# 162 row pairs of the MLP up projections by seven products in place of 120, at other places, in a two-layer decoder trunk

## The chip, the cores and the metric

One core of a Trainium2 chip runs the whole program. The metric is the device time of one execution in microseconds (us). Five engines have queues of their own that run in order: PE (matrix multiply; PEld is its loading of weights), DVE (vector), ACT (scalar), POOL and SP. SP issues almost all DMAs here.

## The reference, cut to what matters

Two layers, 256 tokens, 2048 channels, float32. Each layer is a token mixer (forgetting attention in layer 0, a mixture of dilated windows in layer 1) and an MLP, each behind an RMS norm and added to the residual stream. The change is in the MLPs:

```python
def sq_relu_mlp(h, w_up, w_down):      # h 256 x 2048, w_up 2048 x 8192, w_down 8192 x 2048
    a = jax.nn.relu(h @ w_up)
    return (a * a) @ w_down

h = rms_norm(x, mlp_norm_g[i])
x = x + sq_relu_mlp(h, mlp_w_up[i], mlp_w_down[i])
```

## The kernel before, in words

**Precision.** Each float32 operand is split in two reduced-precision parts, hi and lo (`cut`, L340): ACT casts the weight to hi (L342), DVE subtracts hi from the weight to give lo (L348). A product is three matmuls: hi by hi, hi by lo, lo by hi (L386 to L388).

**Units and blocks.** A `Unit` (L352) is a matrix product of all 256 tokens with 512 columns of a weight; its sums stay in two or four PSUM banks. It runs in eight blocks. A block (L361) is a pair of 128-row chunks of the weight: one 512 KB DMA into a `raw` buffer, a hi and a lo, and PE's work. There are three forms of PE's work:

- `whole` (L376): 12 matmuls of 512 columns.
- `quarters` (L391): the same 12, with the columns in another order, for plain blocks of a unit that also has blocks by seven products.
- `parts` (L410): the 2x2 arrangement (two token halves, two row chunks, two column halves) by seven products in place of eight, 21 matmuls of 256 columns. For this DVE forms sums of weights in a second `raw` buffer (L413, L418, L420), and both the weights (768 columns of them) and the sums (1024 columns) are cut to hi and lo. The sums of tokens (`sigma`, made in `normed` and `sums_of_tokens`) are made once per MLP from each quarter of the normed input.

The table `HALVED` (L42) says for each of the four periods of an MLP and each of the period's four up units which of the eight blocks go by `parts`. Before, it is blocks 0, 2, 4, 5 and 7 in every unit of periods 1 to 3 and none in period 0: 60 pairs per MLP, 120 in all.

**Periods.** In `mlp` (L1016) an MLP is four periods of 2048 of the 8192 inner columns. Period 0 has only four up units. In each later period the four up units alternate with the four down units of the period before, block by block, in an order that a string gives (`UU_D`, L1014: U an up block, D a down block). After the last period come its four down units alone. An up unit ends in `up_end` (L944): ACT moves the banks to a buffer `z` (L968 or L953), DVE adds up the seven products' results there (L973 to L986), ACT applies relu, DVE transposes to `tr` (L994), four DMAs write to DRAM (L448), one reads back into `z` (L453), ACT squares (L1002), and ACT and DVE make hi and lo of the down unit's operand `aT` (L1007, L1009). A down unit ends in an addition to x on DVE (L527).

**Buffers.** They are rings of slots (`Ring`, L62): six `raw`, four `hi`, four `lo`, and in the MLPs more by `MORE` (L41), one of each. `z` has one slot, `tr` four.

**What sets the order.** All steps are recorded with a duration from small formulas (`on_act`, `on_dve`, `moved`, L45 to L54). The planner (`Plan`, L89) plays them through with those durations and hand-over times (`gap`, L137) and emits each engine's instructions in the order that comes out; PE's blocks keep the order in which they were recorded, and steps of attention are set between them. On the chip each engine then runs its own queue in that order.

Of the kernel before, what the change touches and what calls it, by code (L numbers as in the profile page):

```python
# [13 lines left out]
ALU = mybir.AluOpType  # L14
# [3 lines left out]
P = 128  # L18
D = 2048
S = 256  # L20
NT = S // P
NC = 512
# [13 lines left out]
PERIODS = DFF // D  # L36
# [1 line left out]
QUARTER = 0.112  # L38
ADDING = ()
FIVE = (0, 2, 4, 5, 7)  # L40
MORE = (1, 1, 1)  # L41
HALVED = [[(), (), (), ()], [FIVE] * 4, [FIVE] * 4, [FIVE] * 4]  # L42


def on_act(n, accum=False):  # L45
    return 0.24 + 0.00083 * n + (0.19 if accum else 0)


def on_dve(n, inputs=2):
    return 0.17 + (0.00104 if inputs == 2 else 0.00054) * n  # L50


def moved(kb):
    return kb / 380.0  # L54


class Item:
# [31 lines left out]
class Plan:  # L89

    HANDOFF = 0.25
    LANDING = 2.1
    BACKLOG = 2.0
    FIRST = 14.0
# [40 lines left out]
    def gap(self, a, b):  # L137
        if a.eng == "dma":
            return self.LANDING
        if a.eng is None:  # L140
            return 0.0
        if a.eng == b.eng:
            return 0.0 if a.eng == "pe" else 0.06
        return self.HANDOFF

    def order(self, rounds=3):
        for ring in self.rings:
# [81 lines left out]
def trunk(ctx: ExitStack, tc, x, fox_w_in, fox_b_f, fox_q_gain, fox_k_gain, fox_w_out, dil_w_in,  # L229
          dil_q_gain, dil_k_gain, dil_w_out, mix_norm_g, mlp_norm_g, mlp_w_up, mlp_w_down, out):  # L230
    nc = tc.nc
    plan = Plan(["fox", "mlp0", "dil", "mlp1"])
    add = plan.add
    T = {}

    def v(item):
        return T[item.slot if isinstance(item, Item) else item]

    def r(item):
        return v(item).bitcast(F32R)  # L240
# [18 lines left out]
    N_RAW = 6  # L259
    N_HI = 4  # L260
    N_LO = 4
    N_Z = 1
    N_C = 1
    raw_ring = ring("raw", N_RAW, 2 * NC)
# [4 lines left out]
    blocks_ring = Ring(plan, [f"blocks{i}" for i in range(4)])  # L269
    rings = {}  # L270
    for ph in ("mlp0", "mlp1"):
        rings[ph] = dict(sigma=ring("sigma", 4, 2 * 4 * 2 * P, ph), tr=ring("tr", 4, NT * NC, ph),
                         z=ring("z", N_Z, 6 * S, ph), c=ring("c", N_C, NC, ph))
    for ph, n_sets, heads in (("fox", 1, 4), ("dil", 3, 2)):
        rings[ph] = dict(
            s=ring("s", 4, 3 * P, ph), w=ring("w", 4 if ph == "fox" else 3, NT * NC, ph),
# [3 lines left out]
            ph=ring("ph", 2, S, ph), pl=ring("pl", 2, S, ph), pw=ring("pw", 2, P, ph))  # L280
# [194 lines left out]
    def x_keys(n):  # L475
        return [(f"x{n}", t) for t in range(NT)]
# [41 lines left out]
            reads=[room, (sigma, 0)], writes=[(sigma, 1)])  # L518


    def add_to_x(n, then=None):
        def end(banks):
            pair = banks[0].slot[0]

            def go():
# [415 lines left out]
    out_proj(oT, fox_w_out[0], then1)  # L941


    def up_end(l, phase, source, halved):  # L944
        own = rings[phase]

        def end(banks):
            z, turned = own["z"].take(), own["tr"].take()
            by = lambda t: v(f"rstd{l}")[:, t:t + 1]
            if not halved:  # L950
                for t in range(NT):
# [48 lines left out]
            for t in range(NT):  # L1000
# [8 lines left out]
            add("dve", on_dve(2 * NC), lambda: nc.vector.tensor_sub(r(a)[:, 2 * NC:], v(turned), v(a)[:, 0:2 * NC]),  # L1009
                reads=[*((turned, t) for t in range(NT)), *((a, b, 0) for b in range(4))], writes=[(a, b, 1) for b in range(4)])  # L1010
        return end

    AC, BE = ("A0", "A1", "C0", "C1"), ("B0", "B1")
    UU_D = "UUDUDUDUDUDUDUDD"  # L1014

    def mlp(l, layer, phase, source, sigmas, then, last=None):  # L1016
        for weights, name, n in ((raw_ring, "raw", MORE[0]), (hi_ring, "hi", MORE[1]), (lo_ring, "lo", MORE[2])):
            slots = [f"{phase}_{name}{i}" for i in range(n)]
            in_phase[phase].update({s: 2 * NC for s in slots})
            weights.more(slots, phase)  # L1020
        downs = []
        turn = 0
        for b in range(PERIODS):
            a = Source()
            ups = []
            for n in range(4):
                halved = HALVED[b][n]
                banks = AC if halved else ("A0", "A1") if b or n % 2 == 0 else ("B0", "B1")
                ups.append(Unit(source, mlp_w_up[layer], 0, [(b * D + n * NC, NC)], banks,
                                up_end(l, phase, a, halved), halved, sigmas))  # L1030
            if b == 0:
                paired(ups[0], ups[1])
                ups[2].blocks(NP)
                ups[3].blocks(NP)
            else:
                for u, d in zip(ups, downs):
                    for c in UU_D:
                        (u if c == "U" else d).block()
            downs = []
            for n in range(NX):  # L1040
                banks = ("E0", "E1") if turn % 2 == 0 else ("B0", "B1")
                turn += 1
                end = add_to_x(n, then if b == PERIODS - 1 else None)
# [217 lines left out]
```

## Time and profile before

| | |
|---|---|
| median of 3 runs | 2120.92 us (2120.85 to 2121.04) |
| profiled execution | 2121.22 us, of it the span of the program 2119.5 us |
| PE busy | 2109.8 us |
| PEld, DVE, ACT busy | 1888.0, 1669.8, 1266.0 us |
| moved by DMA | 492.93 MB |
| one MLP, periods 0 to 3 | about 381 to 947 us of the span for layer 0 |

The busy time of PE is made of pipelined matmuls whose ends are modelled: a matmul of 512 columns is listed with 379 ns. Its pace is read from the starts in the timeline. In the list of groups, the columns are line, engine, operation, output and inputs, shapes, count, then busy us and mean ns of one, then the engine's idle time before them with what ended it. In a table of windows a cell is busy us and the number of instructions that ran.

### The profile page before, as it was taken

Reading aid. Unit: us, or ns where it says so; the run is one execution under the profiler, and the core shown is the slowest. Engines: PE = TensorE matmul, PEld = TensorE weight load, DVE = VectorE, ACT = ScalarE, POOL = GpSimd, SP = SyncE. Lnnn points to the kernel's source line nnn. Section 1 sums busy time; section 2 is a strip of 40 time slices with the busy share of each in tenths; the row PEclk is TensorE's granted clock in tenths of the full one; section 3 lists DMA queues with packets and bytes.
Section 4 is the critical chain, followed back from the end, with each engine's and each line's share of the span. In section 5 each row is a group of like instructions: output and inputs, shape, how many; then the busy total and the mean of one; then the engine's idle time right before and its main releaser. Section 6 shows DMA issues by size and latency. Waiting matters only on the chain.

```text
span 2119.5 us, 30432 instructions
## 1 busy us (share of the span) xinstructions
PE 2109.8 (100%) x11285; PEld 1888.0 (89%) x11285; DVE 1669.8 (79%) x2092; ACT 1266.0 (60%) x1640; POOL 57.8 (3%) x51
## 2 busy tenths in 40 slices
PE   9999999999999999999999999999999999999999
PEld 7888888889999999998888888888899999999988
DVE  6777777678899899886787777777678898898874
ACT  5555556566666666666555555556666666666652
POOL 1011000000000000000010000000000000000000
PEclk9999999999999999999999999999999999999999
DMA  7777668777767777777786776768767777777773
GB/s 247 233 221 199 212 217 262 240 243 238 228 225 242 241 225 237 245 257 260 227 259 200 235 223 207 249 203 285 237 223 232 249 228 230 248 229 228 248 259 129
DMA packets 336133, 492.93 MB, mean 233 GB/s; under 512 B 21928, under 2 KB 137712, under 8 KB 335984
## 3 DMA queue, kind: packets, MB, share of 16 engines
q1 hardware_dynamic: 335712, 490.86, 72.9%
q8 instruction: 88, 1.44, 0.3%
q14 instruction: 61, 0.50, 0.1%
q10 hardware_dynamic: 272, 0.13, 0.0%
HBM read 455.26 MB, written 35.65 MB: 232 GB/s over the span
## 4 chain that ended last, share of the span: by engine, by line
PE 99%; DMA 0%; SPq 0%; DVE 0%; issue 0%; ACT 0%
PE bank_B L386 11%; PE bank_B L388 11%; PE bank_B L387 11%; PE bank_C L407 9%; PE bank_A L386 7%; PE bank_A L388 7%; PE bank_A L387 7%; PE bank_E L386 7%; PE bank_E L388 7%; PE bank_E L387 7%; PE bank_A L437 3%; PE bank_A L438 3%; PE bank_A L436 3%; PE bank_C L437 2%; PE bank_C L438 2%; PE bank_C L436 2%
## 5 line engine op out<-in xcount | busy, mean ns | idle before, releaser
L342 ACT CAST hi<-raw 128x1024 fp32r<-128x1024 f32 (+1 forms) x720 | 736.0, 1026 | 585.0 <-PE bank_B L388 171.1
L348 DVE TENSOR_TENSOR lo<-raw,hi 128x1024 fp32r<-128x1024 f32 (+1 forms) x720 | 854.7, 1193 | 277.1 <-ACT hi L342 261.7
L386 PE MATMUL bank_A<-hi,hT 128*128 128x512 f32 x552 | 212.0, 384 | 0.0
L388 PE MATMUL bank_A<-hi,hT 128*128 128x512 f32 x552 | 210.3, 381 | 0.0
L387 PE MATMUL bank_A<-lo,hT 128*128 128x512 f32 x552 | 210.2, 381 | 0.0
L386 PE MATMUL bank_B<-hi,aT 128*128 128x512 f32 x520 | 197.5, 380 | 0.5 <-ACT aT L646 0.5
L388 PE MATMUL bank_B<-hi,aT 128*128 128x512 f32 x520 | 197.1, 379 | 0.0
L387 PE MATMUL bank_B<-lo,aT 128*128 128x512 f32 x520 | 197.1, 379 | 0.0
L386 PE MATMUL bank_B<-hi,hT 128*128 128x512 f32 x480 | 183.7, 383 | 0.0
L387 PE MATMUL bank_B<-lo,hT 128*128 128x512 f32 x480 | 181.9, 379 | 0.0
L388 PE MATMUL bank_B<-hi,hT 128*128 128x512 f32 x480 | 181.9, 379 | 0.0
L386 PE MATMUL bank_E<-hi,aT 128*128 128x512 f32 x472 | 179.0, 379 | 0.0
L387 PE MATMUL bank_E<-lo,aT 128*128 128x512 f32 x472 | 178.9, 379 | 0.0
L388 PE MATMUL bank_E<-hi,aT 128*128 128x512 f32 x472 | 178.9, 379 | 0.0
L342 ACT CAST mlp_hi<-raw 128x1024 fp32r<-128x1024 f32 (+1 forms) x108 | 109.7, 1016 | 90.1 <-PE bank_E L388 27.0
L348 DVE TENSOR_TENSOR mlp_lo<-raw,mlp_hi 128x1024 fp32r<-128x1024 f32 (+1 forms) x108 | 127.0, 1176 | 27.7 <-ACT mlp_hi L342 24.1
L407 PE MATMUL bank_C<-hi,hT 128*128 128x512 f32 x430 | 138.5, 379 | 0.0
L388 PEld LDWEIGHTS bank_A<-hi,hT 128*128 128x128 f32 x552 | 104.9, 190 | 15.4 <-DVE hT L711 0.5
L386 PEld LDWEIGHTS bank_A<-hi,hT 128*128 128x128 f32 x552 | 105.1, 190 | 14.0
L387 PEld LDWEIGHTS bank_A<-lo,hT 128*128 128x128 f32 x552 | 105.0, 190 | 14.1
L388 PEld LDWEIGHTS bank_B<-hi,aT 128*128 128x128 f32 x520 | 98.3, 189 | 14.1 <-DVE aT L647 0.2
L386 PEld LDWEIGHTS bank_B<-hi,aT 128*128 128x128 f32 x520 | 98.4, 189 | 13.3 <-ACT aT L646 0.7
(360 smaller groups left out, 4391.7 us busy)
## 6 DMA issues: line engine op xcount, KB each, us to landing
raw<-in_mlp_w_up_dram SPq DMA_DIRECT2D x222, 512.0 KB, 4.5
raw<-in_mlp_w_down_dram SPq DMA_DIRECT2D x222, 512.0 KB, 4.8
raw<-in_fox_w_in_dram SPq DMA_DIRECT2D x96, 512.0 KB, 4.6
raw<-in_dil_w_in_dram SPq DMA_DIRECT2D x192, 256.0 KB, 3.1
blocks<-mlp_tr SPq DMA_DIRECT2D x176, 128.0 KB, 3.6
mlp_z<-blocks SPq DMA_DIRECT2D x44, 512.0 KB, 5.4
mlp_raw<-in_mlp_w_up_dram SPq DMA_DIRECT2D x34, 512.0 KB, 4.5
mlp_raw<-in_mlp_w_down_dram SPq DMA_DIRECT2D x34, 512.0 KB, 4.6
```

The lines of the kernel that those rows point to most:

```text
L342: add("act", on_act(n), lambda: nc.scalar.copy(r(hi)[:, 0:n], v(src)[:, at:at + n]), reads=keys, writes=[hi])
L348: add("dve", on_dve(n), lambda: nc.vector.tensor_sub(r(lo)[:, 0:n], v(src)[:, at:at + n], v(hi)[:, 0:n]), reads=[*keys, hi], writes=[lo])
L386: nc.tensor.matmul(acc, a, h, start=first and i == 0, stop=False)
L387: nc.tensor.matmul(acc, a, l, start=False, stop=False)
L388: nc.tensor.matmul(acc, b, h, start=False, stop=last and i == 1)
L407: nc.tensor.matmul(to, m, w, start=False, stop=False)
L436: nc.tensor.matmul(acc, a(0), w(0, at), start=first and edge & 1 == 1, stop=False)
L437: nc.tensor.matmul(acc, a(0), w(1, at), start=False, stop=False)
L438: nc.tensor.matmul(acc, a(1), w(0, at), start=False, stop=last and edge & 2 == 2)
```

## The change

- `HALVED` is another table. Each MLP now has 81 pairs by seven products, 162 in all: five in the third up unit of period 0, 26 each in periods 1 and 2 (6 or 7 a unit), 24 in period 3 (6 a unit).
- `MORE` goes from (1, 1, 1) to (0, 2, 1): in the MLPs six `raw`, six `hi`, five `lo` slots, where there were seven, five and five.
- `tr` has three slots for four. A new ring `sums` with one slot takes the place of `z` for the up units of period 0 that have no pair by seven products; `z` serves the others.
- `UU_D` is another string: three up blocks stand first, then two down, and three down blocks last.
- The planner's durations are changed (fixed parts of ACT and DVE steps halved, DMAs slower, hand-overs on one engine longer, and 0.2 us or, behind PE, 0.3 us between engines), so the order of all queues is planned anew, in the mixers too.
- Code for additions by DMA is added (`added`, `BY_DMA`, `LOW_BY_DMA`), and switched off.

```diff
-MORE = (1, 1, 1)
-HALVED = [[(), (), (), ()], [FIVE] * 4, [FIVE] * 4, [FIVE] * 4]
+MORE = (0, 2, 1)
+BY_DMA = False
+LOW_BY_DMA = False
+HALVED = [[(), (), (0, 1, 3, 5, 7), ()],
+          [(0, 1, 2, 3, 4, 6, 7), (0, 1, 3, 5, 6, 7), (0, 2, 3, 4, 5, 6, 7), (0, 1, 4, 5, 6, 7)],
...
 def on_act(n, accum=False):
-    return 0.24 + 0.00083 * n + (0.19 if accum else 0)
+    return 0.12 + 0.00083 * n + (0.19 if accum else 0)
...
 def on_dve(n, inputs=2):
-    return 0.17 + (0.00104 if inputs == 2 else 0.00054) * n
+    return 0.085 + (0.00104 if inputs == 2 else 0.00054) * n
...
 def moved(kb):
-    return kb / 380.0
+    return kb / 335.0
...
-    HANDOFF = 0.25
+    HANDOFF = 0.2
...
-            return 0.0 if a.eng == "pe" else 0.06
-        return self.HANDOFF
+            return 0.0 if a.eng == "pe" else 0.12
+        return 0.3 if a.eng == "pe" else self.HANDOFF
...
-        rings[ph] = dict(sigma=ring("sigma", 4, 2 * 4 * 2 * P, ph), tr=ring("tr", 4, NT * NC, ph),
-                         z=ring("z", N_Z, 6 * S, ph), c=ring("c", N_C, NC, ph))
+        rings[ph] = dict(sigma=ring("sigma", 4, 2 * 4 * 2 * P, ph), tr=ring("tr", N_TR, NT * NC, ph),
+                         z=ring("z", N_Z, 6 * S, ph), c=ring("c", N_C, NC, ph), sums=ring("sums", 1, NT * NC, ph))
...
-            add("dma", 0.45, go, reads=[turned], writes=[(blocks, i)])
+            add("dma", 0.5, go, reads=[turned], writes=[(blocks, i)])
...
-            z, turned = own["z"].take(), own["tr"].take()
+            z, turned = own[room].take(), own["tr"].take()
...
-    UU_D = "UUDUDUDUDUDUDUDD"
+    UU_D = "UUUDDUUDUDUDUDDD"
...
-                banks = AC if halved else ("A0", "A1") if b or n % 2 == 0 else ("B0", "B1")
+                banks = (AC if halved else AC[:2]) if b or n % 2 == 0 else BE if halved else BE[:2]
...
-                                up_end(l, phase, a, halved), halved, sigmas))
+                                up_end(l, phase, a, halved, LOW_BY_DMA and n < 3, "z" if b or halved else "sums"), halved, sigmas))
```

Two places of the planned order matter below. The first is on PE, in layer 0's MLP, where the third up unit of period 0 starts (`hT` is the normed input, `mlp_sigma` the sums of tokens). Before:

```order
L388 MATMUL bank_B<-mlp_hi_2630,hT_115 128x512
L386 MATMUL bank_A<-hi_126,hT_112 128x512
L387 MATMUL bank_A<-lo_130,hT_112 128x512
L388 MATMUL bank_A<-hi_126,hT_112 128x512
L386 MATMUL bank_A<-hi_126,hT_112 128x512
```

And with the change:

```order
L394 MATMUL bank_B<-hi_127,hT_115 128x512
L442 MATMUL bank_A<-hi_128,hT_112 128x256
L443 MATMUL bank_A<-lo_130,hT_112 128x256
L444 MATMUL bank_A<-hi_128,hT_112 128x256
L442 MATMUL bank_C<-hi_128,hT_112 128x256
L443 MATMUL bank_C<-lo_130,hT_112 128x256
L444 MATMUL bank_C<-hi_128,hT_112 128x256
L442 MATMUL bank_C<-hi_128,mlp_sigma_2666 128x256
```

The unit's first block is now 21 matmuls of 256 columns and needs the first `sigma` here, two units earlier than before.

The second place is on DVE, in period 1 of the same MLP: from the last reading of a `raw` buffer to the first sum of weights that is read from the buffer's next load. The first row frees the buffer (`raw_122` before), the last reads what was loaded into it meanwhile. Before:

```order
L348 TENSOR_TENSOR lo_132<-raw_122,hi_128 128x1024
L348 TENSOR_TENSOR lo_133<-raw_123,hi_129 128x1024
L418 TENSOR_TENSOR raw_120<-raw_120,raw_125 128x256
L348 TENSOR_TENSOR mlp_lo_2631<-raw_124,mlp_hi_2630 128x1024
L420 TENSOR_TENSOR raw_120<-raw_120,raw_125 128x256
L1009 TENSOR_TENSOR aT_117<-mlp_tr_2624,aT_117 128x1024
L413 TENSOR_TENSOR raw_123<-raw_122 128x512
```

With the change, where the buffer is `raw_121`:

```order
L354 TENSOR_TENSOR mlp_lo_2678<-raw_121,hi_129 128x1024
L419 TENSOR_TENSOR raw_124<-raw_123 128x512
L1004 TENSOR_TENSOR mlp_z_2673<-mlp_z_2673,mlp_c_2674 128x2x256
L1005 TENSOR_TENSOR mlp_z_2673<-mlp_z_2673 128x2x256
L354 TENSOR_TENSOR lo_130<-raw_122,mlp_hi_2676 128x1024
L424 TENSOR_TENSOR raw_124<-raw_124,raw_123 128x256
L419 TENSOR_TENSOR raw_120<-raw_125 128x512
L426 TENSOR_TENSOR raw_124<-raw_124,raw_123 128x256
L354 TENSOR_TENSOR lo_131<-raw_123,mlp_hi_2677 128x768
L424 TENSOR_TENSOR raw_120<-raw_120,raw_125 128x256
L419 TENSOR_TENSOR raw_122<-raw_121 128x512
```

Between the two rows there were five others, three of 1024 columns and two of 256; now there are nine, of 256 to 1024 columns.

More of the change, by code (lines that the diff above doesn't have):

```diff
@@ L261, in trunk @@
     N_LO = 4
+    N_TR = 3
     N_Z = 1
@@ L518, in sums_of_tokens, with added, add_to_x, go @@
             reads=[room, (sigma, 0)], writes=[(sigma, 1)])
-    def add_to_x(n, then=None):
+    def added(to, of, reads, writes, us):
+        add("pool", 1.2, lambda: nc.gpsimd.dma_start(to(), of(), accum_op=ALU.add), reads=[*reads, *writes])
+        add("dma", us, None, reads=reads, writes=writes)
+    def add_to_x(n, then=None, room=None):
         def end(banks):
             pair = banks[0].slot[0]
+            if room is not None:
+                sums = room.take()
+                for t in range(NT):
+                    def go(t=t):
+                        nc.scalar.copy(halves(v(sums)[:, t * NC:(t + 1) * NC], S), by_column(v(banks[t]), S))
+                    add("act", on_act(NC), go, reads=[banks[t]], writes=[(sums, t)])
+                added(lambda: v(f"x{n}"), lambda: v(sums), [(sums, t) for t in range(NT)], x_keys(n), 2.55)
+                return
             def go():
@@ L941, in trunk, with up_end @@
     out_proj(oT, fox_w_out[0], then1)
-    def up_end(l, phase, source, halved):
+    def up_end(l, phase, source, halved, by_dma, room):
         own = rings[phase]
         def end(banks):
-            z, turned = own["z"].take(), own["tr"].take()
+            z, turned = own[room].take(), own["tr"].take()
             by = lambda t: v(f"rstd{l}")[:, t:t + 1]
@@ L1008, in end @@
                 writes=[(a, b, 0) for b in range(4)])
-            add("dve", on_dve(2 * NC), lambda: nc.vector.tensor_sub(r(a)[:, 2 * NC:], v(turned), v(a)[:, 0:2 * NC]),
-                reads=[*((turned, t) for t in range(NT)), *((a, b, 0) for b in range(4))], writes=[(a, b, 1) for b in range(4)])
-        return end
-    AC, BE = ("A0", "A1", "C0", "C1"), ("B0", "B1")
-    UU_D = "UUDUDUDUDUDUDUDD"
+            whole = [(turned, t) for t in range(NT)]
+            low = [(a, b, 1) for b in range(4)]
+            if by_dma:
+                add("act", on_act(2 * NC), lambda: nc.scalar.mul(r(a)[:, 2 * NC:], v(turned), -1.0), reads=whole, writes=low)
+                added(lambda: v(a)[:, 2 * NC:], lambda: v(turned), whole, low, 2.55)
+            else:
+                add("dve", on_dve(2 * NC), lambda: nc.vector.tensor_sub(r(a)[:, 2 * NC:], v(turned), v(a)[:, 0:2 * NC]),
+                    reads=[*whole, *((a, b, 0) for b in range(4))], writes=low)
+        return end
+    AC, BE = ("A0", "A1", "C0", "C1"), ("B0", "B1", "E0", "E1")
+    UU_D = "UUUDDUUDUDUDUDDD"
     def mlp(l, layer, phase, source, sigmas, then, last=None):
@@ L1042, in mlp @@
                 turn += 1
-                end = add_to_x(n, then if b == PERIODS - 1 else None)
+                end = add_to_x(n, then) if b == PERIODS - 1 else add_to_x(n, None, rings[phase]["sums"] if BY_DMA else None)
                 downs.append(Unit(a, mlp_w_down[layer], b * D, [(n * NC, NC)], banks, end, adding=ADDING if b < PERIODS - 1 else ()))
```

2 rows, old and new, of the table HALVED are left out of this document.

## The prediction

> **What bounds the kernel now.** I read the page first: busy times, then the chain that ended last.
>
> ```profile
> PE 2109.8 (100%) x11285; PEld 1888.0 (89%) x11285; DVE 1669.8 (79%) x2092; ACT 1266.0 (60%) x1640; POOL 57.8 (3%) x51
> PE 99%; DMA 0%; SPq 0%; DVE 0%; issue 0%; ACT 0%
> ```
>
> PE ends everything: 99% of the chain is its own, and no other engine releases it for long. What counts is PE's pace, so I read it from starts in the timeline, in layer 0's MLP, at one pair by seven products (the L436 to L438 rows) and the plain pair behind it.
>
> ```profile
> 468.00 0.27 PE L436 MATMUL bank_A<-hi,hT 128*128 128x256 f32 x1
> 468.11 0.28 PE L437 MATMUL bank_A<-lo,hT 128*128 128x256 f32 x1
> ...
> 470.35 0.38 PE L386 MATMUL bank_E<-hi,aT 128*128 128x512 f32 x1
> ...
> 472.94 0.38 PE L407 MATMUL bank_C<-hi,hT 128*128 128x512 f32 x1
> ```
>
> The 21 short matmuls start over 470.35 - 468.00 = 2.35 us, the 12 long ones over 472.94 - 470.35 = 2.59 us: 0.112 and 0.216 us each. The pace holds over whole periods; these are layer 0's four, by windows (the cells are PE, PEld, DVE, ACT, POOL, clock, DMA share, GB/s):
>
> ```profile
> 381.00:463.85 82.85, 82.85 (x396) 72.87 (x396) 57.00 (x61) 49.45 (x59) 0.70 (x1) 1.00 0.76 235
> 463.85:624.74 160.89, 160.89 (x953) 146.84 (x953) 140.70 (x173) 102.43 (x120) 0.00 (x0) 1.00 0.73 234
> 624.74:785.63 160.89, 160.89 (x953) 146.84 (x953) 143.46 (x177) 103.03 (x121) 0.00 (x0) 1.00 0.74 235
> 785.63:946.52 160.89, 160.89 (x942) 146.52 (x942) 141.91 (x171) 102.28 (x120) 0.00 (x0) 1.00 0.76 246
> ```
>
> By finer starts the two pairs are 2.346 us (21 x 0.1117) and 2.588 us (12 x 0.2157). Periods 1 to 3 have 32 up blocks, 20 of them by seven products, and 32 down blocks: 44 x 2.588 + 20 x 2.346 = 160.8 us by pace alone. Each takes 160.89, so PE waits for nothing there. The engine nearest to it is DVE: 87 to 89% in periods 1 to 3, 69% in period 0. The granted clock is 1.00 throughout.
>
> What does DVE do in the 18.9 us per period in which it idles? The waits of DVE over the three periods:
>
> ```profile
> DVE lo L348 <- ACT hi L342: 25.0, 40, 1.1
> DVE raw L413 <- DMA raw<-in_mlp_w_up_dram: 15.9, 16, 1.8
> DVE mlp_lo L348 <- ACT mlp_hi L342: 6.4, 9, 1.0
> DVE raw L413 <- DMA mlp_raw<-in_mlp_w_up_dram: 2.2, 1, 2.2
> DVE mlp_raw L413 <- DMA raw<-in_mlp_w_up_dram: 0.4, 1, 0.4
> ```
>
> 31.4 us are waits for ACT's hi. ACT in turn mostly waited for PE, as its casts of weights show in the groups by shape (the last columns are ACT's idle time and what ended it):
>
> ```profile
> L342 ACT CAST hi<-raw 128x1024 fp32r<-128x1024 f32 x642 | 672.1, 1049 | 515.3 <-PE bank_B L388 155.8 <-PE bank_A L388 119.5 <-PE bank_E L388 79.7
> L342 ACT CAST hi<-raw 128x768 fp32r<-128x768 f32 x78 | 65.2, 836 | 69.6 <-PE bank_E L388 27.0 <-PE bank_B L388 15.3 <-PE bank_C L407 13.8
> ```
>
> It waits for a matmul to free a hi buffer: DVE is ahead of PE there and its idling is harmless. The other 18.5 us, in 18 waits, are of another kind: the first sum of weights waits for the load of those weights, whatever PE does. It is 18.5 / 60 pairs = 0.31 us a pair.
>
> **The change part by part.**
>
> *PE.* 162 - 120 = 42 plain pairs become pairs by seven products: 42 x (2.588 - 2.346) = 10.2 us less. This falls on the chain directly. Ten of the pairs (2.4 us) are in period 0 of the two MLPs, 32 in periods 1 to 3.
>
> The Trainium skill, "TensorE: Matmul & The Clock Gate", section "Back-to-back issue gap", speaks against this: it gives a sustained 81 ns for matmuls of 128 columns and 131 ns for 512. Between them my estimate from that page is 98 ns for 256, and 21 short ones would then cost 0.49 us more than 12 long ones, 20 us over the 42 pairs. The trace does not agree: its spacings are 112 and 216 ns.
>
> *DVE.* Each new pair adds the three sums and a lo of 768 columns. Prices by starts, while DVE is back to back:
>
> ```profile
> 706.62 0.69 DVE L413 TENSOR_TENSOR mlp_raw<-raw 128x512 f32<-128x512 f32 x1
> 707.22 0.69 DVE L985 TENSOR_TENSOR mlp_z<-mlp_z,mlp_c 128x512 f32<-128x512 f32 x1
> ...
> 710.76 1.22 DVE L348 TENSOR_TENSOR lo<-raw,hi 128x1024 fp32r<-128x1024 f32 x1
> 711.90 0.42 DVE L420 TENSOR_TENSOR mlp_raw<-mlp_raw,raw 128x256 f32<-128x256 f32 x1
> 712.23 0.95 DVE L348 TENSOR_TENSOR lo<-raw,hi 128x768 fp32r<-128x768 f32 x1
> 713.10 0.42 DVE L418 TENSOR_TENSOR raw<-raw,raw 128x256 f32<-128x256 f32 x1
> 713.44 1.24 DVE L994 STREAM_TRANSPOSE mlp_tr<-mlp_z 128x1024 f32<-128x1024 f32 x1
> ```
>
> L413 takes 0.60, L420 0.33, the short lo 0.87, L418 0.34: together 2.14 us a pair (the listed 0.42 to 0.95 us overlap). A lo of 1024 columns takes 1.14. In period 0, five pairs are 10.7 us, and the unit's longer end (L973 to L986, three steps of 512 and two of 256 columns, 2.5 us) comes on top, against 25.9 us of idling; they hide. In periods 1 and 2 six more pairs are 12.8 us, in period 3 four are 8.6 us. PE's periods shrink to 159.44, 159.44 and 159.92 us. What is left of idle time on DVE is
>
> - period 1: 159.44 - 140.70 - 12.8 = 5.9 us,
> - period 2: 159.44 - 143.46 - 12.8 = 3.2 us,
> - period 3: 159.92 - 141.91 - 8.6 = 9.4 us.
>
> The waits for ACT can go into this freely: they shrink as DVE falls back towards PE. The waits for loads cannot. At 0.31 us a pair they would be 8.1 us in periods 1 and 2 (26 pairs) and 7.4 in period 3, so 2.2 + 4.9 = 7.1 us too much per MLP, which PE would then wait for. If no wait is left, nothing is lost. These are the ends of the one unknown, 0 and 14.2 us over both MLPs.
>
> *Which value?* A late load comes from the time in which its buffer was freed. The landing times in the list of DMA issues, after the issue:
>
> ```profile
> raw<-in_mlp_w_up_dram SPq DMA_DIRECT2D x222, 512.0 KB, 4.5
> raw<-in_mlp_w_down_dram SPq DMA_DIRECT2D x222, 512.0 KB, 4.8
> ```
>
> DVE work between the freeing and the first sum, with the prices above, is 3 x 1.14 + 2 x 0.34 = 4.1 us at the place shown before, under the landing time: it waits whenever DVE has not idled meanwhile. At the place shown with the change it is 4 x 0.60 + 1.14 + 3 x 0.34 + 0.87 = 5.4 us. Over all pairs of layer 0's MLP the medians are about 4.4 us before and 4.95 now, though the number of `raw` buffers falls from seven to six: the planner has moved the sums of weights back. For plain blocks the distance shrinks (its median from 10.4 to 8.5 us), mostly above the 4.5 to 4.8 us and a cast of 1.05. So I take half a microsecond off each of the 18 waits of 1.03 us: 18 x 0.53 = 9.5 us over 60 pairs, 0.16 a pair. That makes 4.1 us in a period with 26 pairs: nothing too much in period 1, 0.9 in period 2. A few plain loads and sums come late as well; I give them another 1 us a MLP. Both MLPs lose 2 x 1.9 = 3.8 us, nearer to the lower end than to the upper.
>
> The Trainium skill, "DMA: Bandwidth & Descriptors", section "Anatomy of one DMA — SWDGE (gpsimd) path", fits a fixed 2.0 us and bytes over 436 GB/s. An estimate by it is 3.2 us for 512 KB, and by this no load would be late and the 3.8 us would be zero; the trace's 4.5 and 4.8 us speak for the longer.
>
> *ACT* gets one more cast of 768 columns per pair, 0.84 us by the rows above, so 5 us more in a period where it is busy 102 to 103 of 160.9. PE's own work hides it, and it costs nothing unless DVE waits behind it. *Buffers:* hi grows to six where lo has five, so ACT can be one buffer ahead of DVE; this takes away part of the 31 us of waits. The `sums` slot frees `z` for the third unit's products. *DMA:* the same loads; 492.93 MB stay. *Sigma* is needed two units, 41 us, earlier. In the timeline of before the last one of layer 0 is written here:
>
> ```profile
> 403.73 1.22 DVE L517 TENSOR_TENSOR mlp_sigma<-mlp_z,mlp_sigma 128x1024 fp32r<-128x1024 f32 x1
> ```
>
> That is done at 405 us, and the third unit begins 16 x 2.588 = 41 us behind 381, at 422: 17 us are left. *Attention:* its PE steps were planned again with shorter hand-overs, but at least two plain products (2.6 us) still stand between the transposes of probabilities and their use, as before. I take 0, with 1 us to either side.
>
> *Sum.* 2121.2 us of the profiled execution (its span of 2119.5 and 1.7 around it) - 10.2 + 3.8 = 2114.8. The median of the runs lies 0.3 us under that execution: 2114.5 us.
>
> **The rivals.**
>
> 1. *Nothing is lost.* The sums stand late enough for every load, and DVE's buffers take up the rest: 2120.9 - 10.2 = 2110.7 us. For it: PE never waited at 89% DVE, and five lo ahead are 6 to 13 us of PE's work. Against it: 3.2 us of slack in period 2 are 2%.
> 2. *Loads bound DVE.* With six `raw` buffers each first sum still waits as long as now or longer. It turns the change into a loss from 0.26 us a pair: 26 x 0.26 = 6.8 us, so 0.9 and 3.6 us too much in periods 1 and 2, with 1 us more per MLP 11 us. At 0.31 and without that 1 us it is 14.2 us (2125 us). At 0.4 it is 10.4 us a period and 9.6 in period 3: 4.5 + 7.2 + 0.2 per MLP, 24 us, 2135. For it: one `raw` buffer fewer, and more pairs to share them. Against: the longer distances.
> 3. *Half is lost*, 6 to 14 us: waits for ACT that stay although DVE is behind, since a lo of sums follows its own last sum by an ACT cast of about 1.05 us, put a few tenths on each pair. 26 x 0.1 us = 2.6 us in each of four periods are 10 us: 2121 us.
> 4. *Short matmuls are not half a long one.* From 2.588 / 21 = 0.123 us each the new pairs lose; the rows show 0.112. Only at 0.146 would it be the 20 us worked out from the Trainium skill, "TensorE: Matmul & The Clock Gate". By the trace it is hardly possible.
>
> **How the numbers follow.** Forecast (1 to 6 us lost, 2111.7 to 2116.7): 0.44. Rival 1: 0.24. Rival 3 (2116.7 to 2125): 0.18. Rival 2: 0.13. Rival 4: 0.01. A measurement of this kernel can tell about 0.2%, 4.2 us, from no change: faster is under 2116.7, slower over 2125.2. Faster 0.68, same 0.18, slower 0.14. The range, 2110.2 to 2123, leaves out rivals 2 and 4 and a part of rival 3.
>
> **What would show it.** Right: starts of short and long matmuls 0.112 and 0.216 us apart; periods 1 and 2 between 159.4 and 161 us, period 0 81.6 us; DVE at 95 to 99% of periods 1 and 2; its waits for ACT's hi down to a third; first sums (L419) waiting 0.1 to 0.2 us a pair. Rival 2 shows as such waits over 0.26 us a pair, and PE waiting for lo of DVE; rival 3 as waits for hi of the sums. Wrong altogether: PE waiting in attention, or period 0 longer than 82.85 us.

## The result: slower by 1.3%, and the profile after

The changed kernel takes 2149.29 us (median of 4 runs, 2147.34 to 2150.23) against 2120.98 us of the kernel before beside it: a ratio of 1.0131, 95% interval 1.0113 to 1.0148. 2114.5 was forecast.

From the page of the changed kernel, the busy times and the chain of waits:

```profile
PE 2113.6 (98%) x11665; PEld 1896.9 (88%) x11665; DVE 1751.1 (82%) x2270; ACT 1284.8 (60%) x1690; POOL 60.1 (3%) x51
PE 73%; DVE 11%; DMA 9%; issue 4%; ACT 2%; SPq 0%; DVEq 0%; ACTq 0%
```

PE held 99% of the chain before; now a quarter goes through DVE, loads and ACT. Where? By the starts of PE's blocks, layer 0's MLP has these four periods (the cells are PE, PEld, DVE, ACT, POOL, clock, DMA share, GB/s):

```profile
379.21:460.87 81.66, 81.66 (x431) 73.00 (x430) 68.25 (x84) 51.27 (x64) 0.69 (x1) 1.00 0.71 228
460.87:626.90 166.03, 162.54 (x1008) 149.27 (x1007) 149.36 (x192) 105.56 (x128) 0.00 (x0) 0.99 0.71 229
626.90:791.36 164.46, 161.73 (x1008) 147.89 (x1006) 155.81 (x203) 104.91 (x127) 0.00 (x0) 1.00 0.73 237
791.36:954.02 162.66, 160.59 (x988) 147.26 (x987) 148.02 (x184) 104.03 (x125) 0.00 (x0) 1.00 0.73 236
```

Period 0 takes the 81.66 us that its matmuls need, as forecast. Periods 1 to 3 need 159.42, 159.42 and 159.70 us by PE's pace (a run without waits, below, shows it) and take 166.03, 164.46 and 162.66: 14.6 us over. The periods of layer 1's MLP take 83.30, 167.92, 169.04 and 161.56 us by the same starts, 21.6 over in all. The stretches outside the MLPs are 3.1 us longer. By the same windows the MLPs' matmuls themselves take 10.3 us less than before. Together -10.3 + 14.6 + 21.6 + 3.1 = 29.0 us, the difference of the two spans.

What did DVE wait for in these three periods?

```profile
DVE raw L419 <- DMA raw<-in_mlp_w_up_dram: 19.9, 18, 2.8
DVE lo L354 <- ACT hi L348: 9.1, 10, 2.1
DVE lo L354 <- ACT mlp_hi L348: 3.7, 7, 1.2
```

And ACT, whose waits were for PE before (the L342 rows of the prediction)?

```profile
ACT hi L348 <- DVE raw L426: 44.2, 22, 4.4
ACT mlp_hi L348 <- DVE raw L426: 28.9, 17, 3.5
ACT mlp_tr L1021 <- DMA mlp_z<-blocks: 18.2, 10, 2.8
ACT hi L348 <- DMA raw<-in_mlp_w_down_dram: 17.2, 10, 4.5
...
ACT hi L348 <- DMA raw<-in_mlp_w_up_dram: 6.6, 8, 1.8
ACT mlp_hi L348 <- DMA raw<-in_mlp_w_down_dram: 5.8, 3, 4.2
ACT mlp_hi L348 <- DMA raw<-in_mlp_w_up_dram: 3.3, 5, 1.6
```

ACT no longer runs ahead. It waits 73.1 us for DVE's last sums, 32.9 us for loads, those of plain pairs above all, and 18.2 us for the reading back of an up unit's products from DRAM (`mlp_z<-blocks`), for which it waited 1.5 us before. DVE waits 12.8 us for the casts queued behind. One place shows the knot, in the timelines of SP, DVE, ACT and PE:

```profile
557.03 0.37 SPq L341 DMA_DIRECT2D raw<-in_mlp_w_up_dram  x1
...
558.80 1.15 ACT L1021 ACTIVATE mlp_tr<-mlp_z 128x512 f32<-128x512 f32 x2 [1.59 <-DMA mlp_z<-blocks]
...
560.71 0.96 DVE L354 TENSOR_TENSOR lo<-raw,hi 128x768 fp32r<-128x768 f32 x1 [0.50 <-ACT hi L348]
...
561.59 1.05 ACT L348 CAST mlp_hi<-raw 128x1024 fp32r<-128x1024 f32 x1 [0.90 <-DMA raw<-in_mlp_w_down_dram]
...
562.81 0.69 DVE L419 TENSOR_TENSOR raw<-raw 128x512 f32<-128x512 f32 x1 [0.80 <-DMA raw<-in_mlp_w_up_dram]
...
563.88 1.22 DVE L354 TENSOR_TENSOR lo<-raw,mlp_hi 128x1024 fp32r<-128x1024 f32 x1
565.02 1.22 DVE L354 TENSOR_TENSOR mlp_lo<-raw,hi 128x1024 fp32r<-128x1024 f32 x1
566.15 0.42 DVE L426 TENSOR_TENSOR raw<-raw,raw 128x256 f32<-128x256 f32 x1
566.29 0.38 PE L443 MATMUL bank_A<-mlp_lo,mlp_sigma 128*128 128x256 f32 x1 [2.28 <-DVE mlp_lo L354]
566.68 1.04 ACT L348 CAST hi<-raw 128x1024 fp32r<-128x1024 f32 x1 [2.37 <-DVE raw L426]
```

ACT's wait at 558.80 makes the next cast late, for which DVE waits 0.50 us. The load issued at 557.03 is there 5.8 us later; the first sum at the head of DVE's queue starts with it at 562.81, and the two lo of 1024 columns behind it are as late. PE waits 2.28 us for the second, and ACT 2.37 us for the last sum, which comes after both.

### The profile page after: what moved, and what is told of

Same layout as the page of the kernel before. It is cut to its first block, busy times and chain, and to the rows that moved or that the text cites. A ratio compares the mean times of both kernels' runs of the same rounds, so it can differ in the third digit from the quotient of the medians.

```text
span 2148.5 us, 31744 instructions
## 1 busy us (share of the span) xinstructions
PE 2113.6 (98%) x11665; PEld 1896.9 (88%) x11665; DVE 1751.1 (82%) x2270; ACT 1284.8 (60%) x1690; POOL 60.1 (3%) x51
## 4 chain that ended last, share of the span: by engine, by line
PE 73%; DVE 11%; DMA 9%; issue 4%; ACT 2%; SPq 0%; DVEq 0%; ACTq 0%
PE bank_B L392 9%; PE bank_B L393 9%; PE bank_B L394 9%; DMA raw<-in_mlp_w_up_dram 6%; PE bank_A L392 6%; PE bank_A L394 6%; PE bank_A L393 6%; DVE lo L354 6%; PE bank_E L392 5%; PE bank_E L393 5%; PE bank_E L394 5%; PE bank_C L413 3%; PE bank_A L443 2%; DVE mlp_lo L354 2%; PE bank_A L444 2%
## 5 line engine op out<-in xcount | busy, mean ns | idle before, releaser
L354 DVE TENSOR_TENSOR lo<-raw,hi 128x1024 fp32r<-128x1024 f32 (+1 forms) x646 | 758.5, 1183 | 211.4 <-ACT hi L348 178.7
L348 ACT CAST mlp_hi<-raw 128x1024 fp32r<-128x1024 f32 (+1 forms) x226 | 220.2, 993 | 136.3 <-DVE raw L426 61.9
L354 DVE TENSOR_TENSOR lo<-raw,mlp_hi 128x1024 fp32r<-128x1024 f32 (+1 forms) x180 | 204.7, 1149 | 13.5 <-ACT mlp_hi L348 8.7
L392 PE MATMUL bank_A<-hi,hT 128*128 128x512 f32 x480 | 185.0, 385 | 0.0
L394 PE MATMUL bank_A<-hi,hT 128*128 128x512 f32 x480 | 182.7, 381 | 0.0
L392 PE MATMUL bank_B<-hi,aT 128*128 128x512 f32 x460 | 174.6, 380 | 0.0
L394 PE MATMUL bank_B<-hi,aT 128*128 128x512 f32 x460 | 174.3, 379 | 0.0
L419 DVE TENSOR_TENSOR raw<-raw 128x512 f32<-128x512 f32 x162 | 111.3, 687 | 54.8 <-DMA raw<-in_mlp_w_up_dram 54.7
L443 PE MATMUL bank_A<-lo,mlp_sigma 128*128 128x256 f32 x372 | 104.9, 282 | 11.0 <-DVE lo L354 10.8
L354 DVE TENSOR_TENSOR mlp_lo<-raw,hi 128x1024 fp32r<-128x1024 f32 (+1 forms) x90 | 106.0, 1178 | 9.5 <-PE bank_A L393 2.7
L393 PEld LDWEIGHTS bank_E<-lo,aT 128*128 128x128 f32 x520 | 98.8, 190 | 12.9
L394 PEld LDWEIGHTS bank_A<-hi,hT 128*128 128x128 f32 x480 | 91.2, 190 | 13.0
```

The costliest lines, as they stand in the source:

```text
L348: add("act", on_act(n), lambda: nc.scalar.copy(r(hi)[:, 0:n], v(src)[:, at:at + n]), reads=keys, writes=[hi])
L354: add("dve", on_dve(n), lambda: nc.vector.tensor_sub(r(lo)[:, 0:n], v(src)[:, at:at + n], v(hi)[:, 0:n]), reads=[*keys, hi], writes=[lo])
L392: nc.tensor.matmul(acc, a, h, start=first and i == 0, stop=False)
L393: nc.tensor.matmul(acc, a, l, start=False, stop=False)
L394: nc.tensor.matmul(acc, b, h, start=False, stop=last and i == 1)
L419: add("dve", on_dve(2 * q), lambda: nc.vector.tensor_add(v(sums)[:, 0:2 * q].rearrange("p (g n) -> p g n", g=2), v(raw)[:, q:3 * q].rearra ...
```

## The experiments

"Lost" below is what a run's median has over PE's pace: 2121.0 us with 120 pairs, 2110.8 with 162 (2121.0 - 10.2), 2118.6 with 130. The changed kernel loses 38.5 us. The runs are called e1 to e18 in their order here.

### First: which part of the change?

Four theories stood at the start. A: six `raw` buffers in place of seven make the loads late. B: DVE cannot do 26 pairs a period in its order. C: the planner's shorter durations make an order that stalls whatever the table. D: the new block order does.

**The old table in the changed kernel.**

```
-HALVED = [[(), (), (0, 1, 3, 5, 7), ()], ...
+HALVED = [[(), (), (), ()], [FIVE] * 4, [FIVE] * 4, [FIVE] * 4]
```

> The changed kernel with the table of 120 pairs put back; buffers, block order and planner durations stay as changed. Theory A (six raw buffers make the loads of weights late, and late first sums hold up DVE's queue): with 20 pairs a period DVE keeps 18 us idle to absorb them, so PE waits little: 2121 to 2124 us. Theory B (26 pairs a period are more than DVE can do in order): nothing lost, 2120 to 2122 us. Theory C (the planner's shorter durations give an order that stalls by itself): well over 2130 us.

2146.7 us, ratio 1.0123 [1.0107, 1.0138]: 25.7 us lost with as few pairs as before. The pairs are not needed for the loss, so B does not explain it alone.

**The new table alone in the kernel before.**

> The kernel before with the new table of 162 pairs alone: seven raw, five hi, five lo buffers, the old block order and the old durations. A: with seven raw buffers most of the 38 us lost on the changed kernel go, 2112 to 2125 us. B: the loss stays or grows, 2140 to 2160 us. C: as A, since the durations are the old ones.

2151.82 us, 1.0143 [1.0126, 1.0160]: 41 us lost, with seven `raw` buffers. Part of it, at least, is of another kind: PE waits for banks that ACT has not moved out (in the whole run):

```profile
PE bank_A L439 <- ACT mlp_z L971: 15.3, 4, 5.7
```

**The old durations in the changed kernel.**

```
-    return 0.12 + 0.00083 * n + (0.19 if accum else 0)
+    return 0.24 + 0.00083 * n + (0.19 if accum else 0)
...
-    HANDOFF = 0.2
+    HANDOFF = 0.25
```

> The changed kernel with the planner's five old durations and hand-overs. A and B: 2140 to 2160 us, as the changed kernel. C: most of the loss goes, under 2125 us.

2176.32 us, 1.0262 [1.0246, 1.0277], 27 us worse than the change: what C forecast does not come.

This run and the one before it are no clean tests, though. A plan has times of its own, so it also says how long PE is to wait in it. In the MLPs that is nothing in the plans of the kernel before and of the change, but 56.0 us in that of e2 and 59.8 in that of e3. With 162 pairs and the old, longer fixed parts of the steps the planner itself finds no order without waits, whatever the loads do on the chip.

**Seven raw, five hi and five lo buffers** (the change has six, six and five).

```
-MORE = (0, 2, 1)
+MORE = (1, 1, 1)
```

> The changed kernel with the old MLP buffers, seven raw, five hi, five lo instead of six, six, five. A: first sums wait for their loads under 3 us a period where they waited 11.2, 0.8 and 7.9 us in the first MLP, and the time falls under 2125 us. B: 2140 us or more, the waits of DVE move to others. C: 2145 to 2150 us.

2131.89 us, 1.0052 [1.0037, 1.0067]: the seventh buffer brings back 17 of the 38 us. A holds in part.

**Both, the old table and seven buffers.**

> The changed kernel with the table of 120 pairs and the old MLP buffers (seven raw, five hi, five lo); the new block order and durations stay. A (six raw buffers are why 120 pairs lost 26 us): 2120 to 2124 us, no PE wait in the MLPs. D (the block order with three up blocks in a row is why): 2135 us or more.

2139.7 us, 1.0089 [1.0075, 1.0103]: 19 us lost, although the pairs and the raw, hi and lo buffers are as before the change. A alone falls too.

**The old table and the old block order in the changed kernel.**

```
-    UU_D = "UUUDDUUDUDUDUDDD"
+    UU_D = "UUDUDUDUDUDUDUDD"
```

> The changed kernel with the table of 120 pairs and the old block order, but still six raw, six hi, five lo and the new durations. A: the loss stays, 2135 to 2147 us, with first sums waiting 60 us or more for loads. D: 2120 to 2125 us.

2155.4 us, 1.0165 [1.0150, 1.0181], 9 us worse than with the new block order: D falls. The first sums wait 135.7 us for loads in the whole run, as A had it, but the time lies above A's range too.

**Eight raw buffers**, at the cost of one `tr` buffer (`MORE = (2, 1, 1)`, `N_TR = 2`).

> The changed kernel with eight raw, five hi, five lo buffers, paid for by two transposed tiles in place of three; table, block order and durations as changed. A: more than the seven raw buffers gave, 2115 to 2126 us, first sums waiting under 20 us in all where seven gave 42. B (DVE's work of 26 pairs a period is the rest of the loss): as with seven, 2127 to 2135 us.

2141.31 us, 1.0095 [1.0081, 1.0109], worse than with seven. The first sums wait 62.5 us for loads in the whole run, where seven gave 42.6 and under 20 was expected: both forecasts miss. What the lost `tr` buffer does in it was not told apart.

**Only the five pairs of period 0**, in the kernel before.

```
-HALVED = [[(), (), (), ()], [FIVE] * 4, [FIVE] * 4, [FIVE] * 4]
+HALVED = [[(), (), (0, 1, 3, 5, 7), ()], [FIVE] * 4, [FIVE] * 4, [FIVE] * 4]
```

> The kernel before with nothing but five pairs by seven products in the third up unit of period 0 of each MLP: 130 pairs, all buffers, the block order and the durations old. The prediction's price of 0.242 us a pair with DVE's work hidden: 2120.9 - 10 x 0.242 = 2118.5 us. If period 0 cannot hide it: 2121 us or more.

2122.42 us, 1.0008 [0.9999, 1.0017]. Period 0 takes 81.7 us, the 1.2 us less that were priced, and period 1 takes 3.7 us more in layer 0 and 2.4 in layer 1.

So no single part is the culprit. The plans of e1 and of e4 to e8 have PE wait in the MLPs for 1.6 us at most, and on the chip these kernels lose 4 to 34 us. The question became what the plans leave out.

### Then: loads or DVE's work?

**Only the new durations, in the kernel before.**

> Only the planner's five durations of the change are put into the kernel before; 120 pairs, seven raw buffers and the old block order stay. If it is the order planned from the new durations that makes even 120 pairs stall (as 2139.7 us with seven raw buffers, new durations and new block order suggests), PE waits 10 to 25 us and the time is 2131 to 2146 us. If the durations are harmless and what is left must come from the block order, the third tr buffer or the sums buffer, it is 2119 to 2123 us.

2131.95 us, 1.0049 [1.0034, 1.0064]: 11 us lost, but in the profiled run only 3.6 us of it are in the MLPs, by their starts, and 6.0 outside. The time is in the range of the first case, and the place mostly is not the one that it meant.

**Half the bytes of the loads.** The order of every engine is that of the changed kernel, instruction by instruction; only DMAs are shorter.

```
-                src = w[r0:r0 + rows * P, c:c + width].rearrange("(c p) n -> p c n", p=P)
+                n = 1 if raw.half else rows
+                src = w[r0:r0 + n * P, c:c + width].rearrange("(c p) n -> p c n", p=P)
```

> The changed kernel in its own order, but the loads of MLP weights of periods 1 to 3 (down weights: all periods but the last) move one of their two row chunks, so half of those weights are stale; nothing else differs. Theory A (DVE is held by loads that land 4.6 us after their issue): the landing falls towards 3 us, the waits for loads go, and with them most of PE's 36 us of waits: 2112 to 2122 us. Theory B (DVE simply has too much to do in its order): waits for loads turn into nothing that helps, 2140 to 2150 us. If both hold half, 2125 to 2135 us.

2114.59 us, 0.9970 [0.9958, 0.9981]. All eight MLP periods run at PE's pace. Its DMA issues and the one row that is left of DVE's waits for loads in periods 1 to 3 of layer 0:

```profile
raw<-in_mlp_w_up_dram SPq DMA_DIRECT2D x192, 256.0 KB, 2.7
raw<-in_mlp_w_down_dram SPq DMA_DIRECT2D x192, 256.0 KB, 2.6
```

```profile
DVE raw L421 <- DMA raw<-in_mlp_w_up_dram: 0.8, 1, 0.8
```

With loads of 2.7 us in place of 4.6, the same instructions in the same order on DVE keep up with PE. B falls: DVE can do the work. The reading back from DRAM, whose bytes are the same, also takes less here, 4.3 us in place of 5.9, and ACT's waits for it in these periods are 2.9 us in place of 18.2.

**Half the lo of the sums**, again in the changed kernel's own order.

```
-            hi_s, lo_s = cut(sums, [(sums, i) for i in range(3)], 0, 4 * q)
+            hi_s, lo_s = cut(sums, [(sums, i) for i in range(3)], 0, 4 * q, short=2 * q)
```

> The changed kernel in its own order, but the lo of the sums of weights is computed on 512 of its 1024 columns, so half of that lo is stale; DVE has 0.53 us less to do in each of 162 pairs, 13.8 us in a period of 26. Theory B (DVE's work): PE's waits go nearly all, 2110 to 2120 us. Theory A (late loads): the time that DVE gains is spent waiting for the same loads, since each load is issued when its buffer is freed; 2135 to 2149 us.

2123.43 us, 1.0009 [1.0000, 1.0019], between both forecasts: 13.8 us of DVE's work in a period of 26 pairs are gone, and 26 us of the loss. The sums wait longer for loads than in the changed kernel (in periods 1 to 3 of layer 0):

```profile
DVE raw L419 <- DMA raw<-in_mlp_w_up_dram: 30.6, 27, 3.6
```

It is a budget: work and waits share DVE's time, and either may be made smaller. The expectation under A missed that.

**The third sum on GpSimd**, with seven buffers.

```
-            add("dve", on_dve(q), lambda: nc.vector.tensor_add(v(sums)[:, 3 * q:4 * q], ...
+            add("pool", 0.6, lambda: nc.gpsimd.tensor_add(v(sums)[:, 3 * q:4 * q], ...
```

> The changed kernel with seven raw and five hi buffers (2131.9 us before this edit) and the third sum of each pair (128x256) on GpSimd, not DVE; DVE has 0.34 us less in each pair, 8.8 us in a period of 26. Theory B: PE's waits of about 18 us go to under 5, 2112 to 2118 us, faster than before the change. Theory A: as without the edit, 2128 to 2134 us. If GpSimd takes much longer than 1.5 us for a sum, or slows DVE, the lo that follows comes late and the time is over 2135 us.

2176.16 us, 1.0255 [1.0236, 1.0273]. The sums on GpSimd, in the groups by shape:

```profile
L426 POOL TENSOR_TENSOR raw<-raw,raw 128x256 f32<-128x256 f32 x116 | 159.4, 1376 | 703.8 <-DVE raw L424 484.7 <-ACT hi L348 56.2 <-DMA raw<-in_mlp_w_up_dram 37.5
```

A sum takes 1.38 us there and 0.42 on DVE, and the plan counted 0.6 us: again an order made with a duration too short. In layer 0's MLP DVE's lo of 1024 columns also grew from 1.22 to 1.27 us. That these two make the 44 us was not tested apart.

### Last: why do the loads come late?

The planner of the change counts for a load of 512 KB 512 / 335 = 1.53 us and then `LANDING`, 2.1 us: 3.63 us, and up to 2 us more when others are queued before it (its median in the plan is 3.63). The trace of the changed kernel has this (the last number is the median, in us, from issue to landing):

```profile
raw<-in_mlp_w_up_dram SPq DMA_DIRECT2D x256, 512.0 KB, 4.6
raw<-in_mlp_w_down_dram SPq DMA_DIRECT2D x256, 512.0 KB, 4.8
```

**A plan that knows it.** One number of the changed kernel:

```
-    LANDING = 2.1
+    LANDING = 3.2
```

> The changed kernel, planned with 3.2 us for LANDING in place of 2.1, so that a load of 512 KB counts 4.7 us as measured. If the plan's short loads are why sums wait, DVE's order puts them later, the waits for loads go to under 3 us per period and PE waits under 15 us in all: 2112 to 2128 us. If six raw buffers cannot be filled in time in any order, 2140 us or more.

2114.08 us (2111.58 to 2115.02), 0.9967 [0.9954, 0.9980]: with the same 162 pairs, instructions and buffers 3.3 of the 38.5 us of loss are left. The profiled run is the fastest of the five. The chain, three periods of layer 0, and the waits in them of DVE for loads and of ACT for PE and for last sums:

```profile
PE 99%; DMA 0%; DVE 0%; ACT 0%; issue 0%; SPq 0%; DVEq 0%
```

```profile
460.33:619.91 159.58, 159.58 (x1007) 147.38 (x1006) 151.42 (x196) 107.80 (x129) 0.00 (x0) 1.00 0.75 237
619.91:779.33 159.42, 159.42 (x1007) 147.30 (x1006) 154.59 (x199) 105.75 (x126) 0.00 (x0) 1.00 0.76 243
779.33:939.03 159.70, 159.70 (x989) 146.96 (x987) 149.40 (x185) 105.02 (x124) 0.00 (x0) 1.00 0.76 242
```

```profile
DVE raw L419 <- DMA raw<-in_mlp_w_up_dram: 3.9, 5, 1.7
...
ACT hi L348 <- DVE raw L426: 25.8, 20, 3.4
ACT hi L348 <- PE bank_E L394: 22.5, 16, 3.1
ACT hi L348 <- PE bank_B L394: 15.5, 12, 4.1
```

The waits for loads are 3.9 us, not 19.9, ACT waits for PE again, and for the reading back from DRAM only 0.5 us. The loads land hardly sooner (up 4.6 us in both, down 4.6 for 4.8). What differs is the order. In the plan of the change 58 of the 162 first sums stand less than 4.6 us behind the issue of their load, and 27 casts; with 3.2 none does. (In the plan of the kernel before it is 48 of 120 first sums.) A piece of DVE's queue in period 1, lines with - as the change has it, with + as planned with 3.2:

```
-L419 TENSOR_TENSOR raw_121<-raw_120 128x512
 L354 TENSOR_TENSOR lo_133<-raw_125,hi_127 128x1024
-L424 TENSOR_TENSOR raw_121<-raw_121,raw_120 128x256
+L419 TENSOR_TENSOR raw_121<-raw_120 128x512
 L354 TENSOR_TENSOR lo_132<-raw_124,hi_126 128x1024
-L426 TENSOR_TENSOR raw_121<-raw_121,raw_120 128x256
+L424 TENSOR_TENSOR raw_121<-raw_121,raw_120 128x256
 L354 TENSOR_TENSOR mlp_lo_2678<-raw_120,hi_128 128x768
+L426 TENSOR_TENSOR raw_121<-raw_121,raw_120 128x256
```

Here each sum stands one lo later, some 1.1 us, about what was added to `LANDING`, and a lo whose data are there runs first. The rest of the queue is rearranged too, so this piece is an example and not the whole difference.

**The same with seven raw and five hi buffers.**

> As the run with 3.2 us for LANDING, and seven raw, five hi and five lo buffers in place of six, six and five (2131.9 us without the longer LANDING). If buffers and plan add up, 2111 to 2122 us, the best of these; if the plan does not matter, about 2132 us; if raw buffers decide alone, 2132 us here and 2149 us in the run with six.

2112.84 us, 0.9964 [0.9951, 0.9977], not to be told from e13. Once the plan is right, the seventh buffer that was worth 17 us is worth about one.

**Half the bytes of the down loads alone**, none of which is summed, in the changed kernel's own order.

> The changed kernel in its own order; the down loads of all periods but the last move one of their two row chunks (half of those weights are stale), the up loads are whole. If only the landing of the loads that are summed counts, most waits for loads stay, 2135 to 2149 us. If the loads share one stream, so that the up loads land earlier when the downs are short (under 4 us), it falls to 2115 to 2130 us.

2119.78 us, 0.9994 [0.9985, 1.0004]: 29.5 of the 38.5 us come back. The up loads, whole, land in 4.3 us in place of 4.6, and the first sums in layer 0's periods 1 to 3 wait

```profile
DVE raw L421 <- DMA raw<-in_mlp_w_up_dram: 3.8, 6, 1.7
```

So it is not the landing of the summed loads alone. All loads go through one ring of buffers and one queue, and a shorter down load lets ACT cast earlier (its waits for down loads fall from 23.0 to 4.2 us) and its buffer go earlier to the next load. How much is from the queue and how much from the buffers, the run does not separate.

**The five pairs of period 0 with 3.2 us** (e8 and `LANDING`).

> The kernel before with five pairs by seven products in the first period of each MLP and none moved elsewhere (2122.4 us with the old LANDING, 1.2 us gained and 2 to 4 us lost behind it per MLP), planned with 3.2 us for LANDING. If the plan's short loads caused that loss, it keeps the 2.4 us: 2117 to 2119.5 us, under the kernel before. If not, 2121 to 2128 us.

2133.95 us, 1.0064 [1.0047, 1.0081], a miss: 15 us lost. It is one place in each MLP (in layer 0):

```profile
PE bank_E L386 <- ACT aT L1007: 3.4, 1, 3.4
PE bank_E L388 <- DVE aT L1009: 1.4, 1, 1.4
```

PE stands before the last two down blocks of the first unit until the activations of period 0's fourth unit (`aT`) are cut. The timeline of ACT shows when that unit's products (bank_B) left their banks, and what came just before:

```profile
479.92 1.15 ACT L1002 ACTIVATE mlp_tr<-mlp_z 128x512 f32<-128x512 f32 x2
...
482.85 1.25 ACT L953 ACTIVATE mlp_z<-bank_B,rstd 128x512 f32<-128x512 f32 x2
```

Period 0 ended at 460.07, but the products wait 22.8 us for the only `z`, which the third unit with its longer end still holds at 479.92. Late loads are not needed for it: the plan of e16 itself has PE wait 16.7 us in its MLPs, 6.5 of them at this place in each, and that of e8 nothing. The change gives plain units of period 0 the `sums` buffer, and e13, with the same five pairs, does not wait there. The buffer alone was not run.

**The old table, and 3.2 us, in the changed kernel.**

> The changed kernel with 3.2 us for LANDING and the old table of 120 pairs (2146.7 us with 2.1). If the longer LANDING mends this plan as well, only PE's pace is left between it and e13 (2114.1 us): 42 pairs x 0.242 us = 10.2 us more, 2122 to 2127 us. If the table and not the LANDING decides, over 2130 us.

2122.65 us, 1.0009 [0.9999, 1.0018]. PE waits nowhere in its MLPs. Against e13 the 42 pairs are worth 2122.65 - 2114.08 = 8.6 us.

**3.2 us in the kernel before.**

> The kernel before with 3.2 us for LANDING alone. PE waits for nothing in its MLPs, so there is nothing to gain but a microsecond or two in attention: 2118 to 2123 us. If the longer LANDING makes the old durations plan badly, as e16 may show, PE waits 7 to 8 us behind each first period: 2130 to 2137 us.

2120.49 us, 0.9998 [0.9989, 1.0008]: the number brings nothing in a kernel whose PE does not wait.

The pairs of runs that differ in `LANDING` alone, in us:

| | 2.1 us | 3.2 us |
|---|---|---|
| the change | 2149.29 | 2114.08 (e13) |
| the change with seven `raw`, five `hi` | 2131.89 (e4) | 2112.84 (e14) |
| the change with 120 pairs | 2146.70 (e1) | 2122.65 (e17) |
| the kernel before | 2120.92 | 2120.49 (e18) |
| the kernel before with five pairs more | 2122.42 (e8) | 2133.95 (e16) |

The first three plans lose 35, 19 and 24 us to the shorter number. The last loses to the longer one, by waits that stand in its plan.

## Why the prediction was wrong, step by step

- **PE's 10.2 us: right.** The matmuls start as forecast; period 0 takes 81.66 us, and e13 runs its periods 1 to 3 within 0.25 us of the forecast 159.44, 159.44 and 159.92. The 42 pairs bring 8.6 us once nothing else is late.
- **DVE's work: about right.** 149.4, 155.8 and 148.0 us, against 153.5, 156.3 and 150.5 (140.70 + 12.8, 143.46 + 12.8, 141.91 + 8.6; the prediction's windows began 3.4 us into a period, which shifts some work between them). The sum of 453.2 leaves 25.3 us beside the 478.5 of PE's pace.
- **"I take half a microsecond off each of the 18 waits": too small a wait, by 0.1 us a pair.** The first sums wait 19.9 us over 76 pairs, 0.26 a pair, not 0.16. That is the point from which rival 2 counted a loss, and its price there was 11 us.
- **"The waits for ACT can go into this freely: they shrink as DVE falls back towards PE": this step failed**, and with it rival 2's price. The argument took ACT as an engine ahead of DVE. But every pair by seven products has two casts, and the second waits for DVE's last sum, so ACT in its order falls behind with DVE. 12.8 of the 31.4 us of waits for hi remained, and 10.9 are there even in e13, whose MLPs do not stall. They were not free to give way, and took their part of the slack in both runs. By loads alone, as the prediction counted, layer 0 would have lost about 1 us: they took 11.2, 0.8 and 7.9 us in periods 1 to 3, and the slack was 10.1, 3.6 and 11.7. With the waits for hi and 2.9 us of others, DVE's named waits are 35.6 us against 25.3 of slack. That is 10.3 of the 14.6 us that layer 0's MLP lost; the other 4 are not in the list of waits. "A few plain loads and sums come late as well; I give them another 1 us a MLP" was too little as well: ACT waited 32.9 us for loads in the three periods (15.9 in e13).
- **The medians of distances (4.4 us before, 4.95 now) were the wrong measure.** I set them against landings of 4.5 to 4.8 us and found them long enough. A median of distances hides the short ones, and it was the planner's 3.63 us, which the change left some 1 us under the measured landing, that made 58 of 162 of them too short. Single landings are longer still, as the 5.8 us above, and a late sum delays those behind it. That landings which the plan counts too short are the cause is shown from two sides: e13 beside the change (one number, 35 us) and e10 (shorter loads in the same order). Whose landings is not told apart: `LANDING` counts for every DMA, so for the reading back from DRAM too, and that also got faster in e10 and is waited for less in e13.
- **Attention** costs 3.1 us with the stretches around it; 0 with 1 to either side was forecast. e9, the new durations alone, loses 6.0 us there, and the profiled run of e13 only 0.3.
- **The rivals.** The signs of rival 2 are there (0.26 us a pair, PE waiting for lo of DVE), and rival 3's mechanism, casts of sums that DVE must wait for, is part of what happened. But 2149 us lies beyond the price of every rival; the dearest was 2135. Rival 4 did not occur.

What stays open: why layer 1's MLP lost half as much again as layer 0's from the same table, and why the kernel before, planned with loads of 3.45 us, does not stall. It has 18.9 us of idle DVE time a period and seven buffers, but e5 has as few pairs and as many buffers and loses 19 us.

## What to carry to other kernels

Where a planner makes the order, compare the durations that it counts with those of the trace before pricing any change: a load counted 1 us short cost nothing in one order of 120 pairs here, 24 us in another, and 35 us with 162 pairs. Ask the plan, too, for the waits that it foresees: a loss that stands in the plan is another matter than one that comes on the chip. Slack of an in-order engine is not free for new work while its waits are for loads, and its waits for a second engine did not vanish here where that engine itself waited for the first. To tell load time from work, halve the bytes of the loads and leave the order alone.

## What the runs showed of the hardware

A wait of PE can cost more than its length. Behind the wait that ends at 566.29 in the changed kernel (2.65 us from start to start), matmuls start at half the rate for 3.4 us:

```profile
566.77 0.42 PE L443 MATMUL bank_A<-mlp_lo,mlp_sigma 128*128 128x256 f32 x1
566.98 0.42 PE L444 MATMUL bank_A<-hi,mlp_sigma 128*128 128x256 f32 x1
...
568.48 0.63 PE L392 MATMUL bank_E<-mlp_hi,aT 128*128 128x512 f32 x1
568.90 0.63 PE L393 MATMUL bank_E<-lo,aT 128*128 128x512 f32 x1
...
570.14 0.38 PE L393 MATMUL bank_E<-lo,aT 128*128 128x512 f32 x1
570.36 0.38 PE L394 MATMUL bank_E<-mlp_hi,aT 128*128 128x512 f32 x1
```

Short ones are 0.21 us apart and long ones 0.42, then 0.22 again from 570.14. The granted clock is 0.50 from 566.7 to 570.0, and 1.00 around it. It came after the gap of 3.28 us that ends at 1570.23 too, and not after one of 2.66 us that ends at 1670.24. The Trainium skill, "TensorE: Matmul & The Clock Gate", section "Part 1: The HAM clock gate (the "warmup" mystery)", tells of a clock halved after an idle window of about 3.4 us, for about as long. The length of the slow stretch agrees, 3.4 us; a shorter gap, 2.65 us, was enough here once and 2.66 us another time was not. The two stretches cost 1.7 and 1.4 us by the starts, so of the 38.5 us lost the clock is a small part.
